# Six slots of split weight parts instead of four, splits five parts ahead, in a two-layer decoder trunk

## The chip, the cores and the metric

One core of one Trainium2 chip. The time is that of one execution on the device, in microseconds; for the kernel before, the median of three runs is 2111.45 us (2107.8 to 2112.7). Engine names follow the profile: PE is TensorE, DVE is VectorE, ACT is ScalarE, POOL is GpSimd, SP is the engine whose queue issues most loads.

## The reference, cut to what matters

256 tokens of width 2048 go through two layers. Layer 0 mixes tokens with a chunked gated linear attention (GLA), layer 1 with a sliding-window attention (SWA). Both also attend with 4 heads to 256 memory tokens. Each layer ends with an MLP of width 8192. All of it is float32.

```python
mem_n = rmsnorm(mem, mem_norm_g)
for i in range(2):
    h = rmsnorm(x, attn_norm_g[i])
    mk, mv = split(mem_n @ w_mem_kv[i])          # memory keys and values of this layer
    o_mix, xq = gla(h) if i == 0 else swa(h)
    x = x + concat(o_mix, softmax(xq mk) mv) @ w_out[i]
    x = x + square(relu(rmsnorm(x) @ w_up[i])) @ w_down[i]
return rmsnorm(x, final_norm_g)
```

## The kernel before

Weights are read once, as a list of 128 x 1024 float32 blocks (512 KB, "items", some 900 of them), and every product is made from float32r parts: a block is split into a high part `wh` (an ACT copy that rounds, L993) and a low part `wl` (a DVE subtraction, L994), and a product is high by high, high by low and low by high. An item of the up projection (`u`, L724 to L726) has 12 matmuls of 512 columns, an item of the down projection (`d`, L782 to L784) has 6, one of the attention projections (L198, L199) has 8 of 512 columns and 8 of 256.

One loop goes over the items. At step i it issues the load of item i + 8 (SP queue, a ring `wr` of 6 raw blocks), the preparation of item i + 5, the split of item i + 3 into a ring of 4 `wh` and 4 `wl` slots, then the small work that is due at this step (residual adds, norms, attention heads as generators, the hidden activations), then the matmuls of item i. A framework assigns the semaphores and the final order on each engine at build time; it may let an instruction whose inputs are due go ahead of one that stands before it in the source.

The MLP's down projection does seven eighths of its work with a seven-product scheme for 2 x 2 blocks (`FAST`): from four weight blocks B11, B12, B21, B22 it forms sums. B11 is loaded into a tile `sum` of its own and split; `first_sum` (L828, DVE) adds B12 to it, giving T1; after T1's split an accumulating DMA that POOL issues (L825) adds B22 in place, giving T2; after T2's split another adds B21, giving T4. B12's tile `b` gets B22 added by `third_sum` (L831, DVE), giving T3, from the raw block of B22 that stands in the ring. Per group of 44 items there are 16 of `u` woven with 28 of `d` (7 products, 2 halves, 2 pairs), and seven such groups per layer. In source order the two halves and pairs of T1 and T2, named T1-0 to T1-3 and T2-0 to T2-3 here, stand six or seven items apart. `hid_task` (L750 to L763) turns finished `u` into the operands `hid` of the next group's `d`.

```python
    raw[i] = wp.tile([P, 1024], F32, tag="wr", name="wr", bufs=WR)
    ...
    act.activation(hi[i][:, 0:w], r[:, 0:w], AF.Copy)
    dve.tensor_tensor(lo[i][:, 0:w], r[:, 0:w], hi[i][:, 0:w].bitcast(F32), ALU.subtract)
    if h.then:
        h.then(r)
```

Pools: `wp` holds the three rings, `tp` temporaries for the whole run (`u`, `t`, `sq`, `junk` and small ones), `S["phase"].pool` the tiles of one phase (GLA, MLP 0, SWA, MLP 1). Memory keys and values of layer 1 (`mk1`, `mv1`) are made in the GLA phase and lie in `cp`, for the whole run; those of layer 0 lie in the GLA phase's pool.

Of the kernel before, what the change touches and what calls it, by code (L numbers as in the profile page):

```python
# [20 lines left out]
EPS = 1e-5  # L21
XSCALE = 128.0 ** -0.5
WR = 6
LOAD_AHEAD = 8
PREP_AHEAD = 5
SPLIT_AHEAD = 3
MEM_AT = (10, 15)
WARM = 14

# [51 lines left out]
def trunk_kernel(ctx: ExitStack, tc: tile.TileContext, a, out):  # L81
# [150 lines left out]

    def combine(acc, name):

        u = tp.tile([P, T], F32, tag="u", name=name + "_u")
        act.activation(u, acc[:, T:2 * T], AF.Copy)
        t = tp.tile([P, T], F32, tag="t", bufs=4, name=name + "_t")
        dve.tensor_tensor(t, acc[:, 0:T], u, ALU.add)
        return t

# [12 lines left out]
            self.cm.__exit__(None, None, None)  # L253


    mkv = {1: [cp.tile([P, 4, T], F32, name="mk1"), cp.tile([P, 2, 512], F32, name="mv1")]}

    def act_item(src, first, n, key, gain, start=None):

# [47 lines left out]
    def mem_halves(layer):  # L307
        hs = []

        def mv_done(accs):  # L310
            if layer == 0:
                S["mem_r"] = S["mem_st"].spread()
            for t in range(2):
                act.activation(mkv[layer][1][:, t, :], accs[t], AF.Copy, scale=S["mem_st"].tok[:, t:t + 1])

        hs += tm_halves(f"mv{layer}", [a["w_mv"][layer, i] for i in range(8)], 512, lambda: S["ms"], mv_done)
        for c in range(4):
            def mk_done(acc, c=c):
                t = combine(acc, f"mk{layer}{c}")
                dve.tensor_tensor(mkv[layer][0][:, c, :], t, S["mem_r"], ALU.mult)  # L320

            hs += fm_halves(f"mk{layer}{c}", [a["w_mk"][layer, c, i] for i in range(2)], lambda: S["ms"], mk_done)
        return hs
# [39 lines left out]
    def gla_halves():  # L363
# [29 lines left out]
        def proj_done(job, idx):  # L393
            kind, h, j = job

            def f(acc):
                pool = S["phase"].pool
                if idx == 0:
                    S["r"] = S["st"].spread()
                    S["os"] = {}  # L400
                t = combine(acc, f"p{idx}")
                if kind == "k":
                    if j == 0:
                        S["kT", h] = pool.tile([P, 2, T], F32, tag="kT", name=f"kT{h}", bufs=2)
                    dve.tensor_tensor(S["kT", h][:, j, :], t, S["r"], ALU.mult)
                elif kind == "q":
                    if j == 0:
                        S["qT", h] = pool.tile([P, 2, T], F32, tag="qT", name=f"qT{h}", bufs=2)
                    dve.scalar_tensor_tensor(S["qT", h][:, j, :], t, 1.0 / 16, S["r"], ALU.mult, ALU.mult)
                    if j == 1:  # L410
                        tasks.append(gla_task(h))
                elif kind == "g":
                    sg = tp.tile([P, T], F32, tag="t", bufs=4, name=f"sg{idx}")
                    dve.tensor_tensor(t, t, S["r"], ALU.mult)

                    act.activation(sg, t, AF.Abs)
                    act.activation(sg, sg, AF.Exp, scale=-1.0)
                    act.activation(sg, sg, AF.Ln, bias=1.0)
                    dve.scalar_tensor_tensor(sg, t, 0.0, sg, ALU.min, ALU.subtract)
                    act.activation(sg, sg, AF.Exp)  # L420
                    dve.tensor_tensor(sg, t, sg, ALU.mult)
                    dve.scalar_tensor_tensor(sg, S["on", h][:, j, :], o_gain[:, j:j + 1], sg, ALU.mult, ALU.mult)
                    put_out(3 * h + j, sg)
                else:
                    xq = pool.tile([P, T], F32, tag="xq", name=f"xq0{h}", bufs=2)
                    dve.tensor_tensor(xq, t, S["r"], ALU.mult)
                    tasks.append(xattn_task(0, h, xq))
            return f

        for idx, job in enumerate(GLA_ORDER):  # L430
            if idx == 4:
                hs += mem_halves(0) + mem_halves(1)
            for h in fm_halves(f"p{idx}", [a["w_gla"][idx, i] for i in range(2)], lambda: S["xs"], proj_done(job, idx)):
                hs.append(h)
                if extra and idx < 4:
                    hs.append(extra.pop(0))
# [15 lines left out]
    def gla_task(h):  # L452
# [21 lines left out]
        xb = tmp("gl_xb", [P, 2])  # L474
        dve.tensor_tensor(xb, cs[:, :, 0, 127], cs[:, :, 0, 63], ALU.subtract)
        dve.tensor_scalar(xb, xb, 1.0 / 16, None, ALU.mult)
        ex = tp.tile([P, 2, P], F32, tag="t", bufs=4, name=f"ex{h}")
        for c in range(2):
            act.activation(ex[:, c, :], cs[:, c, 1, :], AF.Exp, bias=xb[:, c:c + 1], scale=1.0 / 16)
        be = e.rearrange("p (c t i) -> p c t i", c=2, t=2)  # L480
# [29 lines left out]
        for j in range(3):  # L510
# [3 lines left out]
            pe.matmul(b[:, P:T], S["v"][:, 1, col:col + P], at[:, T:T + P], start=False, stop=True,  # L514
                      skip_group_check=True)
            act.activation(on[:, j, :], b[:, 0:T], AF.Copy)
            sq.append(tp.tile([P, T], F32, tag="sq", name=f"gsq{h}{j}", bufs=2))
# [8 lines left out]
        inv_sqrt(f"go{h}", b[:, 0:T], 1.0 / 384, r, *[tp.tile([P, T], F32, tag="t", bufs=4, name=f"go{h}_{z}") for z in "vw"])  # L526
        yield
        for j in range(3):
            dve.tensor_tensor(on[:, j, :], on[:, j, :], r, ALU.mult)
# [3 lines left out]
    def start_swa():  # L533
# [12 lines left out]
        S["kd"] = [pool.tile([P, T], F32, name=f"kd{g}") for g in range(3)]  # L546
        S["vt"] = pool.tile([P, 2, 256], F32, name="vt")
        S["os"] = {}

    def kv_task(c, t):  # L550

# [146 lines left out]
    def mlp_halves(layer):  # L698
# [89 lines left out]
        def down_fast(e):  # L788


            def block(pair, u, name):
                return wd[layer, e, 2 * pair + int(name[2]) - 1, 2 * u + int(name[1]) - 1]

            def item(idx, u, pair):
# [17 lines left out]
                        later.append([1, take])  # L812

                def tile_of(kind):
                    return lambda *_: held[kind, pair, u]

                def new(kind):
                    def f():
                        held[kind, pair, u] = S["phase"].pool.tile([P, 1024], F32, tag=f"{kind}{pair}{u}",
                                                                   name=f"{kind}{layer}{e}{pair}{u}")  # L820
                        return held[kind, pair, u]
                    return f

                def plus(other):
                    return lambda raw: pool_e.dma_start(held["sum", pair, u], block(pair, u, other), accum_op=ALU.add)  # L825

                def first_sum():
                    dve.tensor_tensor(held["sum", pair, u], held["sum", pair, u], held["b12", pair, u], ALU.add)  # L828

                def third_sum(raw):  # L830
                    dve.tensor_tensor(held["b12", pair, u], held["b12", pair, u], raw, ALU.add)  # L831
# [122 lines left out]


    S["phase"] = Phase("gla")
    mkv[0] = [S["phase"].pool.tile([P, 4, T], F32, name="mk0"), S["phase"].pool.tile([P, 2, 512], F32, name="mv0")]
    S["xs"] = split_slot("A", "ax0")
    x = [[None] * 4, [None] * 4]
    tasks.append(x_task())  # L960
# [21 lines left out]
    def split(i):  # L982
# [5 lines left out]
        if h.split:  # L988
            h.split(r)
            return  # L990
        hi[i] = wp.tile([P, 1024], F32R, tag="wh", name="wh", bufs=4)
        lo[i] = wp.tile([P, 1024], F32R, tag="wl", name="wl", bufs=4)
        act.activation(hi[i][:, 0:w], r[:, 0:w], AF.Copy)  # L993
        dve.tensor_tensor(lo[i][:, 0:w], r[:, 0:w], hi[i][:, 0:w].bitcast(F32), ALU.subtract)  # L994
        if h.then:
# [84 lines left out]
def _build(a):  # L1080
    import concourse.bacc as bacc

    nc = bacc.Bacc("TRN2", target_bir_lowering=False, num_devices=1, dynamic_dma_scratch_size=8192)
    arrays, aps = {}, {}
    for name, v in a.items():
        arrays[f"in_{name}_dram"] = v
# [14 lines left out]
```

## Time and profile before

| | |
|---|---|
| median of the runs | 2111.45 us |
| the profiled execution | 2112.66 us, its span 2110.9 us |
| PE busy | 2073.6 us, 98% of the span |
| DVE, ACT busy | 1629.5 us (77%), 1252.2 us (59%) |
| granted TensorE clock of the core | 0.998 |
| data moved | 457.32 MB, mean 217 GB/s |

A matmul's busy time in the profile is the time from its start to its end in a pipeline, so the next one can start before it ends; the distance between two starts tells how fast PE goes. Idle time before an instruction and what ended it stand in brackets in a timeline.

### The profile page before, as it was taken

The page shows a single profiled execution, that of the slowest core. Times are in us where ns is not written, and L with a number is a line of the kernel's source. Part 1 is how long each engine was busy: PE and PEld are TensorE (multiplying, and loading weights), DVE is VectorE, ACT ScalarE, POOL GpSimd, SP SyncE. Part 2 cuts the span into 40 slices and gives each one's busy share as a digit, 9 for nine tenths or more (in the row PEclk, how much of TensorE's full clock was granted, in tenths as well). Part 3 has the DMA queues.
Part 4 walks back from the last instruction along what each step waited for, and adds up shares of the span by engine and source line. Part 5 has one row for each costly group of instructions (what it writes and reads, how often), then busy time and mean ns, then how long its engine had stood idle before and what let it go on. Part 6 is the DMA issues. An engine that isn't in the chain of part 4 may idle for free.

```text
span 2110.9 us, 27104 instructions
## 1 busy us (share of the span) xinstructions
PE 2073.6 (98%) x9902; PEld 1719.4 (81%) x9902; DVE 1629.5 (77%) x1993; ACT 1252.2 (59%) x1654; POOL 104.8 (5%) x138
## 2 busy tenths in 40 slices
PE   9999999999999999999999999999999999999998
PEld 9988888888787887877888887787787787877886
DVE  5655787556887988889887688557798887988975
ACT  6644666555666665666656466545566566665664
POOL 0000000000100101101000000000010100101100
PEclk9999999999999999999999999999999999999999
DMA  8856555566879879788776544575987879879773
GB/s 296 286 169 185 171 161 157 174 193 217 231 229 278 227 240 268 219 279 222 227 222 205 173 136 124 164 231 175 267 219 266 233 232 282 223 237 259 224 225 138
DMA packets 128150, 457.32 MB, mean 217 GB/s; under 512 B 14492, under 2 KB 14704, under 8 KB 128016
## 3 DMA queue, kind: packets, MB, share of 16 engines
q1 hardware_dynamic: 109872, 393.40, 56.8%
q0 software_dynamic: 16320, 58.81, 14.9%
q10 hardware_dynamic: 1824, 3.38, 0.5%
q8 instruction: 77, 1.26, 0.2%
q14 instruction: 57, 0.47, 0.1%
HBM read 453.24 MB, written 2.10 MB: 216 GB/s over the span
## 4 chain that ended last, share of the span: by engine, by line
PE 49%; issue 35%; DMA 9%; DVE 3%; ACT 2%; POOL 1%; SPq 0%; POOLq 0%; ACTq 0%; DVEq 0%
DMA sum<-in_w_down_dram 6%; PE p_acc L198 4%; PE s_acc L198 3%; PE u_acc L725 3%; PE u_acc L726 3%; PE u_acc L724 3%; DMA wr<-in_w_down_dram 3%; PE d L783 3%; PE d L782 3%; PE d L784 3%; DVE wl L994 2%; PE p_acc L199 2%; PE s_acc L199 2%; PE o_acc L224 1%; PE o_acc L225 1%
## 5 line engine op out<-in xcount | busy, mean ns | idle before, releaser
L994 DVE TENSOR_TENSOR wl<-wr,wh 128x1024 fp32r<-128x1024 f32 (+1 forms) x626 | 749.3, 1207 | 246.5 <-ACT wh L993 241.6
L993 ACT ACTIVATE wh<-wr 128x1024 fp32r<-128x1024 f32 (+1 forms) x626 | 651.6, 1047 | 435.9 <-PE o_acc L226 85.7
L725 PE MATMUL u_acc<-wl,mx 128*128 128x512 f32 x1024 | 400.3, 391 | 13.5 <-DVE wl L994 13.5
L724 PE MATMUL u_acc<-wh,mx 128*128 128x512 f32 x1024 | 399.8, 391 | 1.4 <-ACT wh L993 1.4
L726 PE MATMUL u_acc<-wh,mx 128*128 128x512 f32 x1024 | 398.7, 389 | 0.0
L993 ACT ACTIVATE wh<-sum 128x1024 fp32r<-128x1024 f32 x224 | 237.9, 1062 | 252.9 <-PE u_acc L726 160.6
L994 DVE TENSOR_TENSOR wl<-sum,wh 128x1024 fp32r<-128x1024 f32 x224 | 273.0, 1219 | 80.8 <-ACT wh L993 80.3
L783 PE MATMUL d<-wl,hid 128*128 128x512 f32 x784 | 309.7, 395 | 9.2 <-DVE wl L994 9.0
L782 PE MATMUL d<-wh,hid 128*128 128x512 f32 x784 | 308.5, 394 | 0.4 <-ACT hid L762 0.4
L784 PE MATMUL d<-wh,hid 128*128 128x512 f32 x784 | 304.5, 390 | 0.0
L725 PEld LDWEIGHTS u_acc<-wl,mx 128*128 128x128 f32 x1024 | 192.3, 188 | 58.8 <-DVE wl L994 19.5
L724 PEld LDWEIGHTS u_acc<-wh,mx 128*128 128x128 f32 x1024 | 192.1, 188 | 42.5 <-ACT wh L993 2.2
L726 PEld LDWEIGHTS u_acc<-wh,mx 128*128 128x128 f32 x1024 | 192.2, 188 | 39.9
L198 PE MATMUL p_acc<-ax,wh 128*128 128x512 f32 x512 | 183.9, 402 | 0.0
L783 PEld LDWEIGHTS d<-wl,hid 128*128 128x128 f32 x784 | 147.4, 188 | 44.5 <-DVE wl L994 15.6
L782 PEld LDWEIGHTS d<-wh,hid 128*128 128x128 f32 x784 | 147.2, 188 | 33.5 <-ACT hid L762 1.2
L784 PEld LDWEIGHTS d<-wh,hid 128*128 128x128 f32 x784 | 147.2, 188 | 32.3
L825 POOL DMA_DIRECT2D sum<-in_w_down_dram x112 | 95.6, 853 | 1496.3 <-DVE wl L994 1274.8
L199 PE MATMUL p_acc<-ax,wl 128*128 128x256 f32 x512 | 143.6, 281 | 0.0
L198 PEld LDWEIGHTS p_acc<-ax,wh 128*128 128x128 f32 x512 | 96.2, 188 | 23.7 <-ACT wh L993 1.0
L198 PE MATMUL s_acc<-ax,wh 128*128 128x512 f32 x304 | 111.3, 407 | 0.0
L831 DVE TENSOR_TENSOR b<-b,wr 128x1024 f32<-128x1024 f32 x56 | 68.3, 1220 | 45.9 <-DMA wr<-in_w_down_dram 45.9
(252 smaller groups left out, 2708.0 us busy)
## 6 DMA issues: line engine op xcount, KB each, us to landing
wr<-in_w_up_dram SPq DMA_DIRECT2D x256, 512.0 KB, 4.6
wr<-in_w_down_dram SPq DMA_DIRECT2D x144, 512.0 KB, 5.0
sum<-in_w_down_dram POOLq DMA_DIRECT2D x112, 512.0 KB, 9.7
wr<-in_w_gla_dram SPq DMA_DIRECT2D x64, 512.0 KB, 3.7
wr<-in_w_out_dram SPq DMA_DIRECT2D x64, 512.0 KB, 3.6
sum<-in_w_down_dram SPq DMA_DIRECT2D x56, 512.0 KB, 4.6
b<-in_w_down_dram SPq DMA_DIRECT2D x56, 512.0 KB, 5.1
wr<-in_w_swa_dram SPq DMA_DIRECT2D x38, 512.0 KB, 3.7
```

The costliest lines, as they stand in the source:

```text
L198: pe.matmul(acc, wh[:, k * P:(k + 1) * P], rk, start=kk == 0, stop=False, skip_group_check=True)
L199: pe.matmul(acc[:, T:2 * T], wl[:, k * P:(k + 1) * P], rk[:, 0:T], start=False, stop=kk == NK - 1, skip_group_check=True)
L724: pe.matmul(acc, hi, h, start=2 * i + k == 0, stop=False)
L725: pe.matmul(acc, hi, l, start=False, stop=False)
L726: pe.matmul(acc, lo, h, start=False, stop=2 * i + k == NK - 1)
L782: pe.matmul(acc, hi, h, start=first and c == 0, stop=False, skip_group_check=True)
L783: pe.matmul(acc, hi, l, start=False, stop=False, skip_group_check=True)
L784: pe.matmul(acc, lo, h, start=False, stop=last and c == 1, skip_group_check=True)
L825: return lambda raw: pool_e.dma_start(held["sum", pair, u], block(pair, u, other), accum_op=ALU.add)
L831: dve.tensor_tensor(held["b12", pair, u], held["b12", pair, u], raw, ALU.add)
L993: act.activation(hi[i][:, 0:w], r[:, 0:w], AF.Copy)
L994: dve.tensor_tensor(lo[i][:, 0:w], r[:, 0:w], hi[i][:, 0:w].bitcast(F32), ALU.subtract)
```

## The change

The rings of `wh` and `wl` get six slots instead of four, and an item is split five steps ahead of its matmuls instead of three, prepared seven instead of five and loaded eleven instead of eight. The raw ring keeps its 6 blocks. The room comes from four places. The temporaries `u`, `t` and `sq` move from `tp` to the pools of the phases that use them. Layer 1's memory keys and values are computed before layer 0's, written to DRAM by two DMAs from ACT's queue and read back by two at the start of the SWA phase. Their tiles share tags with those of layer 0. POOL's scratch for DMA descriptors goes from 8192 to 4096 bytes per partition. Tiles of the seven-product scheme are looked up by group (`e`) too, since the next group's loads are now issued earlier in the source.

```diff
-LOAD_AHEAD = 8
-PREP_AHEAD = 5
-SPLIT_AHEAD = 3
+LOAD_AHEAD = 11
+PREP_AHEAD = 7
+SPLIT_AHEAD = 5
+SLOTS = 6
...
-        u = tp.tile([P, T], F32, tag="u", name=name + "_u")
+        u = S["phase"].pool.tile([P, T], F32, tag="u", name=name + "_u", bufs=3)
...
-        t = tp.tile([P, T], F32, tag="t", bufs=4, name=name + "_t")
+        t = S["phase"].pool.tile([P, T], F32, tag="t", bufs=4, name=name + "_t")
...
-    mkv = {1: [cp.tile([P, 4, T], F32, name="mk1"), cp.tile([P, 2, 512], F32, name="mv1")]}
+    mkv = {}
+    dp = ctx.enter_context(tc.tile_pool(name="dp", bufs=1, space=bass.MemoryType.DRAM))
+    kept = [dp.tile([P, 1024], F32, name=f"kept_{n}") for n in ("mk", "mv")]
+
+    def new_mkv(layer):
+        pool = S["phase"].pool
+        mkv[layer] = [pool.tile([P, 4, T], F32, tag="mk", name=f"mk{layer}"),
+                      pool.tile([P, 2, 512], F32, tag="mv", name=f"mv{layer}")]
+
+    def flat(layer, i):
+        return mkv[layer][i].rearrange("p a b -> p (a b)")
+
+    def keep_mkv():
+
+        for i in range(2):
+            act.dma_start(kept[i], flat(1, i))
+
+    def fetch_mkv():
+        new_mkv(1)
+        for i in range(2):
+            act.dma_start(flat(1, i), kept[i])
...
-            if layer == 0:
+            if layer == 1:
                 S["mem_r"] = S["mem_st"].spread()
+            new_mkv(layer)
...
                 dve.tensor_tensor(mkv[layer][0][:, c, :], t, S["mem_r"], ALU.mult)
+                if (layer, c) == (1, 3):
+                    keep_mkv()
...
-                hs += mem_halves(0) + mem_halves(1)
+                hs += mem_halves(1) + mem_halves(0)
...
         S["os"] = {}
+        fetch_mkv()
...
-                    return lambda *_: held[kind, pair, u]
+                    return lambda *_: held[kind, pair, u, e]
...
-        hi[i] = wp.tile([P, 1024], F32R, tag="wh", name="wh", bufs=4)
-        lo[i] = wp.tile([P, 1024], F32R, tag="wl", name="wl", bufs=4)
+        hi[i] = wp.tile([P, 1024], F32R, tag="wh", name="wh", bufs=SLOTS)
+        lo[i] = wp.tile([P, 1024], F32R, tag="wl", name="wl", bufs=SLOTS)
...
-    nc = bacc.Bacc("TRN2", target_bir_lowering=False, num_devices=1, dynamic_dma_scratch_size=8192)
+    nc = bacc.Bacc("TRN2", target_bir_lowering=False, num_devices=1, dynamic_dma_scratch_size=4096)
```

## Rows read from the trace of the kernel before

**Rows 1.** The page: the span and part 1, busy time, share of the span and instructions of each engine.

```profile
span 2110.9 us, 27104 instructions
PE 2073.6 (98%) x9902; PEld 1719.4 (81%) x9902; DVE 1629.5 (77%) x1993; ACT 1252.2 (59%) x1654; POOL 104.8 (5%) x138
```

**Rows 2.** Who PE waited for in the whole run: total us, times, longest.

```profile
PE u_acc L725 <- DVE wl L994: 13.5, 12, 1.2
PE d L783 <- DVE wl L994: 9.0, 13, 1.6
PE v_acc L224 <- ACT wh L993: 2.2, 2, 1.3
PE u_acc L724 <- ACT wh L993: 1.4, 2, 0.7
```

**Rows 3.** Busy time by stage: GLA, SWA, MLP 0, MLP 1. After the stretch come its length, the engines' busy time with their instructions, the granted TensorE clock, the DMA share and GB/s.

```profile
60.00:460.00 400.00, 400.00 (x2101) 341.36 (x2100) 262.96 (x421) 225.97 (x382) 3.84 (x10) 1.00 0.60 185
1120.00:1410.00 290.00, 290.00 (x1571) 236.33 (x1570) 200.55 (x379) 161.11 (x337) 2.43 (x6) 1.00 0.54 163
460.00:1120.00 660.00, 647.91 (x2894) 530.38 (x2893) 553.02 (x549) 404.96 (x418) 47.78 (x56) 1.00 0.81 237
1410.00:2095.00 685.00, 672.67 (x3000) 550.36 (x2999) 571.13 (x572) 416.17 (x438) 47.79 (x56) 1.00 0.79 234
```

**Rows 4.** PE's timeline at the two waits of one group of 44 items (the second group of MLP 0): start, duration, instruction, idle before.

```profile
652.00 0.39 PE L784 MATMUL d<-wh,hid 128*128 128x512 f32 x1
652.23 0.40 PE L782 MATMUL d<-wh,hid 128*128 128x512 f32 x1
653.52 0.51 PE L783 MATMUL d<-wl,hid 128*128 128x512 f32 x1 [0.90 <-DVE wl L994]
653.87 0.40 PE L784 MATMUL d<-wh,hid 128*128 128x512 f32 x1
...
658.93 0.39 PE L724 MATMUL u_acc<-wh,mx 128*128 128x512 f32 x1
660.45 0.50 PE L725 MATMUL u_acc<-wl,mx 128*128 128x512 f32 x1 [1.13 <-DVE wl L994]
```

**Rows 5.** DVE's timeline ahead of these waits.

```profile
626.84 2.48 DVE L994 TENSOR_TENSOR wl<-sum,wh 128x1024 fp32r<-128x1024 f32 x2
...
636.12 1.23 DVE L994 TENSOR_TENSOR wl<-sum,wh 128x1024 fp32r<-128x1024 f32 x1 [0.80 <-ACT wh L993]
...
639.94 1.23 DVE L994 TENSOR_TENSOR wl<-sum,wh 128x1024 fp32r<-128x1024 f32 x1 [1.45 <-ACT wh L993]
...
651.11 1.23 DVE L831 TENSOR_TENSOR b<-b,wr 128x1024 f32<-128x1024 f32 x1 [2.47 <-DMA wr<-in_w_down_dram]
652.25 2.35 DVE L994 TENSOR_TENSOR wl<-wr,wh 128x1024 fp32r<-128x1024 f32 x2
...
655.32 1.22 DVE L994 TENSOR_TENSOR wl<-wr,wh 128x1024 fp32r<-128x1024 f32 x1
657.23 2.02 DVE L763 TENSOR_TENSOR hid<-q,hid 128x1792 fp32r<-128x1792 f32 x1 [0.69 <-ACT hid L762]
659.17 1.22 DVE L994 TENSOR_TENSOR wl<-wr,wh 128x1024 fp32r<-128x1024 f32 x1
```

**Rows 6.** ACT's timeline (the copies of T2-2 and T2-3), and SP's issue of the load that L831 waits for.

```profile
635.03 1.06 ACT L993 ACTIVATE wh<-sum 128x1024 fp32r<-128x1024 f32 x1 [1.56 <-DMA sum<-in_w_down_dram]
638.84 1.06 ACT L993 ACTIVATE wh<-sum 128x1024 fp32r<-128x1024 f32 x1 [2.75 <-DMA sum<-in_w_down_dram]
...
643.46 0.33 SPq L976 DMA_DIRECT2D wr<-in_w_down_dram  x1
```

**Rows 7.** POOL's timeline: issues of accumulating DMAs, the first two of T1 (T1-2, T1-3), the others of T2.

```profile
625.48 0.85 POOL L825 DMA_DIRECT2D sum<-in_w_down_dram  x1 [3.15 <-DVE wl L994]
628.34 0.85 POOL L825 DMA_DIRECT2D sum<-in_w_down_dram  x1 [2.02 <-DVE wl L994]
629.61 0.85 POOL L825 DMA_DIRECT2D sum<-in_w_down_dram  x1 [0.42 <-DVE wl L994]
633.80 0.85 POOL L825 DMA_DIRECT2D sum<-in_w_down_dram  x1 [3.34 <-DVE wl L994]
```

**Rows 8.** Busy time in one group, from its first accumulating DMA to that of the next group; columns as in rows 3.

```profile
619.20:705.65 86.45, 84.43 (x377) 69.10 (x377) 74.99 (x75) 53.26 (x55) 6.82 (x8) 1.00 0.84 243
```

**Rows 9.** DVE's timeline in the later part of the same group: its idle times there.

```profile
669.84 1.23 DVE L994 TENSOR_TENSOR wl<-sum,wh 128x1024 fp32r<-128x1024 f32 x1 [1.44 <-ACT wh L993]
...
673.93 1.23 DVE L994 TENSOR_TENSOR wl<-sum,wh 128x1024 fp32r<-128x1024 f32 x1 [1.13 <-ACT wh L993]
...
679.40 1.23 DVE L994 TENSOR_TENSOR wl<-sum,wh 128x1024 fp32r<-128x1024 f32 x1 [1.37 <-ACT wh L993]
...
683.77 0.69 DVE L809 TENSOR_TENSOR x<-d,x 128x512 f32<-128x512 f32 x1 [1.77 <-PE d L784]
```

**Rows 10.** ACT's waits in the group of rows 8.

```profile
ACT wh L993 <- PE u_acc L726: 11.1, 7, 1.7
ACT wh L993 <- DMA sum<-in_w_down_dram: 6.1, 3, 2.8
```

**Rows 11.** The page, parts 3 and 6: the queue of POOL's transfers (packets, MB, share of 16 engines), and the accumulating DMA (count, KB, median us to landing).

```profile
q0 software_dynamic: 16320, 58.81, 14.9%
...
sum<-in_w_down_dram POOLq DMA_DIRECT2D x112, 512.0 KB, 9.7
```

**Rows 12.** The busiest 50 us of the SWA phase (columns as in rows 3), and the DMAs that ACT's queue issues for x (min, median, max ns of an issue).

```profile
1250.00:1300.00 50.00, 50.00 (x327) 39.29 (x326) 42.62 (x109) 32.11 (x90) 0.00 (x0) 1.00 0.44 127
...
L297 ACTq DMA_DIRECT2D x<-in_x_tok_dram x8: 334/334/460, 1.3 to 21.1; - x8
```

More of the change, by code (lines that the diff above doesn't have):

```diff
@@ L412, in f @@
                 elif kind == "g":
-                    sg = tp.tile([P, T], F32, tag="t", bufs=4, name=f"sg{idx}")
+                    sg = S["phase"].pool.tile([P, T], F32, tag="t", bufs=4, name=f"sg{idx}")
                     dve.tensor_tensor(t, t, S["r"], ALU.mult)
@@ L476, in gla_task @@
         dve.tensor_scalar(xb, xb, 1.0 / 16, None, ALU.mult)
-        ex = tp.tile([P, 2, P], F32, tag="t", bufs=4, name=f"ex{h}")
+        ex = S["phase"].pool.tile([P, 2, P], F32, tag="t", bufs=4, name=f"ex{h}")
         for c in range(2):
@@ L516, in gla_task @@
             act.activation(on[:, j, :], b[:, 0:T], AF.Copy)
-            sq.append(tp.tile([P, T], F32, tag="sq", name=f"gsq{h}{j}", bufs=2))
+            sq.append(S["phase"].pool.tile([P, T], F32, tag="sq", name=f"gsq{h}{j}", bufs=2))
             act.activation(sq[j], b[:, 0:T], AF.Square)
@@ L525, in gla_task @@
         r = tmp("gl_r", [P, T])
-        inv_sqrt(f"go{h}", b[:, 0:T], 1.0 / 384, r, *[tp.tile([P, T], F32, tag="t", bufs=4, name=f"go{h}_{z}") for z in "vw"])
+        inv_sqrt(f"go{h}", b[:, 0:T], 1.0 / 384, r, *[S["phase"].pool.tile([P, T], F32, tag="t", bufs=4, name=f"go{h}_{z}") for z in "vw"])
         yield
@@ L814, in tile_of @@
                 def tile_of(kind):
-                    return lambda *_: held[kind, pair, u]
+                    return lambda *_: held[kind, pair, u, e]
                 def new(kind):
                     def f():
-                        held[kind, pair, u] = S["phase"].pool.tile([P, 1024], F32, tag=f"{kind}{pair}{u}",
+                        held[kind, pair, u, e] = S["phase"].pool.tile([P, 1024], F32, tag=f"{kind}{pair}{u}",
                                                                    name=f"{kind}{layer}{e}{pair}{u}")
-                        return held[kind, pair, u]
+                        return held[kind, pair, u, e]
                     return f
                 def plus(other):
-                    return lambda raw: pool_e.dma_start(held["sum", pair, u], block(pair, u, other), accum_op=ALU.add)
+                    return lambda raw: pool_e.dma_start(held["sum", pair, u, e], block(pair, u, other), accum_op=ALU.add)
                 def first_sum():
-                    dve.tensor_tensor(held["sum", pair, u], held["sum", pair, u], held["b12", pair, u], ALU.add)
+                    dve.tensor_tensor(held["sum", pair, u, e], held["sum", pair, u, e], held["b12", pair, u, e], ALU.add)
                 def third_sum(raw):
-                    dve.tensor_tensor(held["b12", pair, u], held["b12", pair, u], raw, ALU.add)
+                    dve.tensor_tensor(held["b12", pair, u, e], held["b12", pair, u, e], raw, ALU.add)
                 if name == "B11":
@@ L956, in trunk_kernel @@
     S["phase"] = Phase("gla")
-    mkv[0] = [S["phase"].pool.tile([P, 4, T], F32, name="mk0"), S["phase"].pool.tile([P, 2, 512], F32, name="mv0")]
     S["xs"] = split_slot("A", "ax0")
```

## The prediction

> **What bounds the kernel now.** I read the page first, then PE's waits, then the stages one by one, then the timelines of one group of 44 items on each engine. The page says that PE is busy for 98% of the span [rows 1]. So a change can win only what PE waits for, and PE's waits have few causes: 25 of the 29 are for a `wl` that DVE had not finished, 22.5 us in all, and the rest are two short waits for `wh` and two in the first microseconds [rows 2]. By stage they lie in one place. In the GLA and SWA phases PE is busy for the whole stretch, in the two MLPs it lacks 12.1 and 12.3 us [rows 3]. The granted clock is 1.00 in all four, so nothing is to be had or lost there.
>
> The timelines show why DVE is late in an MLP. Each group has up to two waits, some 7 us apart [rows 4]. Going back from them on DVE [rows 5]: at 651.11 it runs the last `third_sum`, after 2.47 us of waiting for the raw block, and two splits stand behind it (652.25). SP issued that block's load at 643.46 [rows 6], when a slot of the raw ring came free, and it landed 7.6 us later. The slot came late because the splits before it were late: ACT's copies of T2-2 and T2-3 stood still for 1.56 and 2.75 us until accumulating DMAs landed [rows 6]. The one for T2-3 was issued at 628.34 [rows 7], right after T1-3's split, and landed at about 638.8. From the end of T1-3's split (626.84 + 2.48 less an overlapping third split, about 628.1) to the start of T2-3's copy there are 10.8 us, whatever DVE does. Four `d` and two `u` lie between, which PE does in 11.0 us (at 0.23 us from start to start [rows 4], `d` is 1.38 us, `u` 2.76 us), and copy and subtraction take 2.3 us more. So this chain of latency eats some 2 us of whatever DVE is ahead; the late block and `hid` (2.02 us at 657.23, with 0.69 of idle) eat the rest. It is a shortage of cover in one third of the group, not of throughput: DVE is busy for 75.0 of 86.5 us [rows 8], and later in the same group it stands idle because the four slots are full [rows 9]; ACT stands 11.1 us waiting for PE to free one [rows 10].
>
> **The slots, the main term.** How late is DVE? PE wanted the first late `wl` at 652.23 + 0.23 = 652.46 and started on it at 653.52, 1.06 us late; the next matmul started 0.35 us after that instead of 0.23. The second was wanted at 659.16 and started at 660.45, 1.29 us late although PE had already lost 1.2 [rows 4]. Without any wait the second `wl` would be 2.5 us late. That is the cover that this group lacks.
>
> With six slots the copy of item k may start when PE ends item k - 6 instead of k - 4. The two items between are a `d` and a `u` in most places, 1.38 + 2.76 = 4.1 us, and two `d` in some, 2.8 us. Both are more than 2.5 us. DVE must have idle time to run that far ahead: in the later part of the group it has 1.44 + 1.13 + 1.37 + 1.77 = 5.7 us [rows 9], more than 4.1. And over a group without waits, 86.5 less 2.6 = 83.9 us, DVE's 75.0 us and the idle time that slots can't take away (2.47 for the block, 0.80 + 1.45 for T2, 0.69 for `hid` [rows 5]; 5.4 us) make 80.4 us. It still fits, with 3.5 us to spare. So I take it that the waits for `wl` go.
>
> Their price: 22.5 us of idle time [rows 2]. A recorded idle time counts from the modelled end of the matmul before, so a wait cost 1.06 where 0.90 is recorded, and 0.12 more on the next start: 0.28 us for each of 25, 7.0 us. The two waits of `u` for `wh` I take for ACT behind a full ring too; by the same count 1.4 + 0.6 = 2.0 us. Together 31.5 us; the waits at the start (2.2 us) stay, as the first loads set them.
>
> I don't take all of it. The groups differ, and in the first group of each MLP the ring starts from another state; the margin is 1.6 us where `d` and `u` alternate and 0.3 us where two `d` follow each other. I leave 3.5 us, a tenth, standing: 28 us are won. The lower bound of this term is nothing (the chain only moves), the upper 31.5.
>
> **Loads earlier in the source.** SP's loads keep their order, and the raw ring keeps 6 blocks, so a load still waits for the split of the sixth raw block before it. It comes earlier only because that split does. Nothing is added: 0 us, with the last-mentioned load moved forward along with DVE. If it did not move, the 2.47 us at L831 would grow by what DVE gained; this is the second rival.
>
> **Memory keys through DRAM.** Four DMAs of 512 KB on ACT's queue, at 0.33 us to issue each [rows 12]: 1.3 us of ACT, which is busy for 32 of 50 us even in the densest part of SWA. The write must wait for DVE's last product of `mk`, with ACT's next copy queued behind it, and that copy has five items of lead; layer 0's values, which reuse the tile, come eight items later. The read is issued when the SWA phase opens, and the first head that needs it comes four items and two steps after. An item of the attention phases has 16 matmuls, at 400 us / 2101 [rows 3] some 3 us, so six of them, 18 us, cover it. A transfer of this size lands in 4 to 10 us here [rows 11]. Taken: 0. If the cover were gone: each 1 MB at SWA's 127 GB/s for a 0.44 share, that is 290 GB/s when full, is 3.6 us, twice, 7 us at most.
> The Trainium skill speaks against counting it as free: DMA: Bandwidth & Descriptors, section "Issuing engines are not separate DMA queues", says that transfers issued by ScalarE run on the same 16 DMA engines as SyncE's and interleave with them. By that the weights' loads pay for the 2 MB, and the sum would be 21 us won instead of 28; the DMA share of 0.44 to 0.60 in these phases is why I don't follow it here, and no run yet shows it.
>
> **Temporaries, names, order of memory layers.** The same instructions on the same engines; only addresses and the pool change. A phase's tiles now lie over those of the phase before, as others did; all their readers are done by then. 0 us, with 1 us per phase change (four of them) as the bound if one has to wait.
>
> **Half the descriptor scratch.** POOL's issue takes 0.85 us with up to four accumulating DMAs in flight (those of 625.48 to 633.80, the first landing at about 635.0 [rows 6, 7]), and what ended its idle time was always DVE. So no shortage shows. 0 us taken; what a shortage would cost is the third rival.
> By the Trainium skill (DMA: Bandwidth & Descriptors, sections "Terms" and "SWDGE vs HWDGE vs iDMA") a descriptor has 16 bytes and these rings lie in the reserved part of SBUF, so 4096 bytes are an estimated 256 entries, against 9 packets per engine and transfer from the page's count of 16320 for some 118 transfers: 4 in flight would use 36. No run shows what a full ring does.
>
> **The sum.** 2112.66 us less 28 is 2084.7 for an execution like the profiled one, which stands 1.2 us above the median of the runs; less these, 2083.5, say 2084.
>
> **The rivals.**
> *Part of it only.* The framework orders DVE again at build time. If it puts `third_sum` or `hid` in front of more splits than now, or DVE cannot use the 5.7 us, half of the waits stay: 2112 - 14 = 2098. For it: the row at 651.11, where an instruction that waits stands in front of two splits [rows 5]. Against it: the lead now has 1.6 us to give.
> *It moves with the chain.* T1 to T2 stays 10.8 us, the block's 7.6 us too. If DVE's extra lead is spent on waiting there each time, PE's waits stay as they are: 2111. Against it: DVE's idle time is elsewhere [rows 9] and a chain that starts 4.1 us earlier ends 4.1 us earlier.
> *Slower, by the scratch.* If the halved room holds fewer than four transfers, each issue waits for a landing: four of T1 at 10 us apart instead of 1.3 to 4. T2-3's data then come some 20 us later; 6 us of cover leave 14 us, 14 groups, about 200 us: 2280. It decides at fewer than four in flight; with room for three it would be nearer to 3 us a group, 42 against 28, 2126.
> *Slower, by order.* Small work of a step now stands behind two more splits. In the densest SWA stretch DVE is busy for 42.6 of 50 us [rows 12]; if it falls behind there, probabilities reach PE late, by up to two splits (2.4 us), for 12 pairs of heads at two places each: 58 us against 28 gained, 2142. It decides when DVE is more than the three steps behind that the generators leave. Against it: PE doesn't wait once there now, and DVE has 15% left.
>
> **How the numbers follow.** Waits mostly gone (won 18 to 33 us, 2079 to 2094): 0.62. Part only (5 to 18 us, 2094 to 2106): 0.17. Within 0.2%, 4.2 us, which is about what a measurement of this kernel can tell: 0.09, the second rival with some mishaps. Slower: 0.12, of which the scratch 0.04. The range from 2078 to 2104 holds the first case and nearly all of the second. Faster 0.79, same 0.09, slower 0.12.
>
> **What would show it.** PE's waits for `wl` should fall from 25 to a few, and PE's matmuls in the MLPs keep 0.23 us from start to start; the MLPs should give nearly all of the gain, GLA and SWA none. ACT's waits for PE stay, since full slots are the normal state. DVE's wait at L831 and ACT's for accumulating DMAs may stay or grow without PE waiting. POOL's issue should stay at 0.85 us. The prediction is wrong if PE waits in SWA, for `hid`, or for `wl` at the same two places.

## The result: 1% faster, and what stands behind it

| | before | after |
|---|---|---|
| median of the runs | 2110.76 us (2107.8 to 2112.7, 4 runs) | 2090.57 us (2087.34 to 2091.28, 4 runs) |
| the profiled execution, its span | 2112.66, 2110.9 us | 2087.34, 2085.6 us |

The ratio is 0.9903, with a 95% interval from 0.9885 to 0.992. The sign was forecast, and the time lies in the range, but 6.6 us above the forecast: 20.2 us were won by the medians (25.3 by the two profiled executions), not 28.

The page of after, the span and part 1, answers to [rows 1]:

```profile
span 2085.6 us, 27140 instructions
PE 2068.6 (99%) x9902; PEld 1719.9 (82%) x9902; DVE 1625.0 (78%) x1993; ACT 1240.2 (59%) x1654; POOL 104.9 (5%) x138
```

The engines do the same work, so the gain is time that PE no longer stands idle. Who PE waited for in after (total us, times, longest), against [rows 2]; line numbers have moved by 24 or 25 in the MLP, L750 here is L725 there, L808 is L783:

```profile
PE v_acc L225 <- ACT wh L1017: 2.3, 2, 1.9
PE d L808 <- DVE wl L1018: 2.3, 4, 0.8
PE u_acc L750 <- DVE wl L1018: 1.9, 2, 1.0
PE warm L118 <- DVE ones L109: 1.1, 1, 1.1
```

25 waits for `wl` with 22.5 us have become six with 4.2, and the two of `u` for `wh` are gone. The stages (GLA, SWA, MLP 0, MLP 1; columns as in [rows 3]) show PE busy all through GLA and SWA, as before, and lacking 2.1 and 2.5 us in the MLPs in place of 12.1 and 12.3. The granted clock stays at 1.00:

```profile
60.00:460.00 400.00, 400.00 (x2106) 341.87 (x2105) 263.75 (x422) 226.73 (x384) 3.80 (x10) 1.00 0.60 188
1110.00:1400.00 290.00, 290.00 (x1572) 236.26 (x1571) 199.24 (x380) 162.50 (x340) 2.43 (x6) 1.00 0.53 166
460.00:1110.00 650.00, 647.91 (x2904) 532.46 (x2903) 553.67 (x552) 400.35 (x419) 47.88 (x56) 1.00 0.81 242
1400.00:2070.00 670.00, 667.55 (x2985) 548.20 (x2983) 564.76 (x565) 406.00 (x431) 47.84 (x56) 1.00 0.79 236
```

Idle time doesn't show the whole price of a late `wl`. A better measure of an MLP is its length in the trace, from the start of its first matmul of `u` to the start of its last of `d`. This is worked out from the start times of PE's matmuls, for both MLPs together (each rounded to 0.1 us before they are added), and stands below for every kernel. GLA is the time from PE's first instruction to the first `u`, SWA that from the end of MLP 0 to the start of MLP 1. Beside them stand the recorded waits for `wl` and what DVE waited for the raw block in front of `third_sum`. The last column is read off DVE's order, for the last `third_sum` of each group: how many splits run after it though the source has them before it, the split of its own block among them. All of it is of the profiled executions.

| kernel | MLPs, us | GLA | SWA | PE for `wl` | DVE at `third_sum` | splits that `third_sum` is ahead of |
|---|---|---|---|---|---|---|
| before | 1379.0 | 467.9 | 241.9 | 22.5, 25 times | 45.9, 17 times | 3 |
| after | 1354.9 | 467.0 | 242.3 | 4.2, 6 times | 51.6, 16 times | 4 |
| `room_only` | 1375.2 | 466.9 | 242.3 | 19.2, 23 times | 48.7, 23 times | 3 |
| `slots_not_order` | 1352.9 | 466.7 | 242.1 | 1.9, 3 times | 55.7, 17 times | 4 |
| `five_slots` | 1346.7 | 468.6 | 242.3 | none | 18.9, 16 times | 2 |
| `raw_ring` | 1358.2 | 466.5 | 242.3 | 1.0, twice | 1.8, twice | 6 (11 in the first group of an MLP) |
| `pinned_before` | 1348.0 | 467.7 | 241.9 | none | none | 0 |
| `swap_before` | 1348.2 | 468.1 | 241.9 | none | none | 0 (1 in the first group of an MLP) |
| `pinned_room` | 1348.1 | 466.7 | 242.3 | none | none | 0 |
| `pinned_slots3` | 1345.9 | 466.7 | 242.1 | none | none | 0 |
| `pinned_five` | 1346.0 | 468.7 | 242.3 | none | none | 0 |
| `pinned_six` | 1346.0 | 466.8 | 242.3 | none | none | 0 |

So 24.1 us of the 25.3 between the profiled executions lie in the MLPs, and the MLPs had 33.0 us to give (1379.0 less 1346.0). After leaves 8.9 of them. GLA's length goes with the code of that phase: 467.7 to 468.1 us in the old kernel's three, 466.5 to 467.0 in the changed ones with four or six slots. The 468.6 and 468.7 with five slots are a matter of TensorE's clock in these two executions: from 9 to 14 us the granted clock is 0.66 in both, and 1.00 in `pinned_six` and in before. The two are 1.8 and 1.9 us behind `pinned_six` by 15 us, and still so at 281 us.

Why are 8.9 us left? DVE's timeline in one group of MLP 0 of after, at 807 to 825 us (start, duration, instruction, idle before and what ended it), against [rows 5]:

```profile
807.43 1.22 DVE L1018 TENSOR_TENSOR wl<-wr,wh 128x1024 fp32r<-128x1024 f32 x1
811.71 1.23 DVE L856 TENSOR_TENSOR b<-b,wr 128x1024 f32<-128x1024 f32 x1 [3.07 <-DMA wr<-in_w_down_dram]
812.86 3.49 DVE L1018 TENSOR_TENSOR wl<-wr,wh 128x1024 fp32r<-128x1024 f32 x3
...
821.90 2.03 DVE L788 TENSOR_TENSOR hid<-q,hid 128x1792 fp32r<-128x1792 f32 x1 [0.70 <-ACT hid L787]
823.84 2.35 DVE L1018 TENSOR_TENSOR wl<-b,wh 128x1024 fp32r<-128x1024 f32 x2
```

PE's timeline of after behind that:

```profile
825.11 0.50 PE L808 MATMUL d<-wl,hid 128*128 128x512 f32 x1 [0.84 <-DVE wl L1018]
825.45 0.39 PE L809 MATMUL d<-wh,hid 128*128 128x512 f32 x1
```

And SP's timeline, the issue of the block's load:

```profile
804.13 0.33 SPq L1000 DMA_DIRECT2D wr<-in_w_down_dram  x1
```

The last `third_sum` of the group (L856, which was L831) still waits for its raw block, now 3.07 us, and now three splits stand behind it, where two stood before [rows 5], beside the split of its own block (818.51 to 819.73 here, 655.32 there). The three run back to back at 812.86, though ACT had made the last of their copies by 807.95. SP issued the block's load at 804.13 and it landed 7.6 us later, as before [rows 6]. In every group DVE's new lead is spent at this one instruction: the idle in front of it is 3.1 to 4.5 us in after's 14 groups, 2.2 to 3.5 in before's (from the end of the DVE instruction ahead to its start). The lead can be counted, from the end of an item's split to the start of the first matmul that wants its `wl`. The last item split ahead of this `third_sum` has 2.7 to 6.3 us in after's groups, the first one behind it 0.1 to 2.1, and in ten of the 14 groups one of the next eleven items is left with 0.1 us, no more than at a recorded wait. After `hid` at 821.90 the next `wl` comes just too late for PE at 825.11. The six recorded waits with what hangs on them make 5.9 of the 8.9 us; the rest are starts that come late by some 0.1 us each, without recorded idle time.

### The profile page after: what moved, and what is told of

The parts are those of the page before. It is cut to its first block, busy times and chain, and to the rows that moved or that the text cites. A ratio compares the mean times of both kernels' runs of the same rounds, so it can differ in the third digit from the quotient of the medians.

```text
span 2085.6 us, 27140 instructions
## 1 busy us (share of the span) xinstructions
PE 2068.6 (99%) x9902; PEld 1719.9 (82%) x9902; DVE 1625.0 (78%) x1993; ACT 1240.2 (59%) x1654; POOL 104.9 (5%) x138
## 4 chain that ended last, share of the span: by engine, by line
PE 63%; issue 23%; DMA 6%; DVE 6%; ACT 1%; POOL 1%; SPq 0%; ACTq 0%; DVEq 0%; POOLq 0%
PE u_acc L750 6%; PE u_acc L751 6%; PE u_acc L749 6%; PE d L808 5%; PE d L807 5%; PE d L809 5%; PE p_acc L199 4%; DMA sum<-in_w_down_dram 4%; PE s_acc L199 3%; DVE wl L1018 3%; PE p_acc L200 2%; DMA wr<-in_w_down_dram 2%; PE s_acc L200 2%; PE o_acc L225 1%; PE o_acc L226 1%
## 5 line engine op out<-in xcount | busy, mean ns | idle before, releaser
L750 PE MATMUL u_acc<-wl,mx 128*128 128x512 f32 x1024 | 399.0, 390 | 1.9 <-DVE wl L1018 1.9
L808 PE MATMUL d<-wl,hid 128*128 128x512 f32 x784 | 309.3, 395 | 2.3 <-DVE wl L1018 2.3
L750 PEld LDWEIGHTS u_acc<-wl,mx 128*128 128x128 f32 x1024 | 192.3, 188 | 42.7 <-DVE wl L1018 3.0
L808 PEld LDWEIGHTS d<-wl,hid 128*128 128x128 f32 x784 | 147.4, 188 | 34.6 <-DVE wl L1018 5.8
L856 DVE TENSOR_TENSOR b<-b,wr 128x1024 f32<-128x1024 f32 x56 | 68.3, 1220 | 51.6 <-DMA wr<-in_w_down_dram 51.6
```

Of the source, the lines that this page charges most:

```text
L750: pe.matmul(acc, hi, l, start=False, stop=False)
L808: pe.matmul(acc, hi, l, start=False, stop=False, skip_group_check=True)
L856: dve.tensor_tensor(held["b12", pair, u, e], held["b12", pair, u, e], raw, ALU.add)
```

## The experiments

The theory after this look: DVE's order sets the waits. In source order `third_sum` stands behind the split of its own block, item 26 of the group of 44 (counted from 0). At build time it was put further ahead on DVE, and ready splits wait with it. The rivals: the slots themselves fall short (too few, or too few raw blocks), or the chain of accumulating DMAs is late whatever DVE does.

**`room_only`: after, with the rings and distances of before.**

```diff
-LOAD_AHEAD = 11
-PREP_AHEAD = 7
-SPLIT_AHEAD = 5
-SLOTS = 6
+LOAD_AHEAD = 8
+PREP_AHEAD = 5
+SPLIT_AHEAD = 3
+SLOTS = 4
```

> All that makes the room (memory keys through DRAM, temporaries in their phase, half the descriptor scratch, layer 1's memory work first), but four slots and splits, preparation and loads 3, 5 and 8 ahead as before. Theory (cover): the gain comes from the slots alone, so this stands at the time before, 2111 us, within 4 us, and PE waits some 25 times for wl. Rival (order): any change of the source gives the engines another order at build time, and that is what helped: nearer to 2090 us. Rival (cost): the DRAM round trip or the halved scratch costs something that the slots hid: 2115 to 2125 us.

Measured: 2107.9 us (2105.94 to 2111.39, 10 runs), ratio 0.999, from 0.9981 to 0.9999. PE's waits:

```profile
PE u_acc L750 <- DVE wl L1018: 13.8, 12, 1.2
PE d L808 <- DVE wl L1018: 5.4, 11, 1.0
PE u_acc L749 <- ACT wh L1017: 1.4, 2, 0.7
```

The DRAM round trip, the temporaries and the halved scratch cost nothing that can be measured; the pattern of waits is that of [rows 2]. The 2.6 us are hardly more than the interval; `pinned_room` comes back to them.

**`five_slots`: less of the same change.**

```diff
-LOAD_AHEAD = 11
-PREP_AHEAD = 7
-SPLIT_AHEAD = 5
-SLOTS = 6
+LOAD_AHEAD = 10
+PREP_AHEAD = 6
+SPLIT_AHEAD = 4
+SLOTS = 5
```

> The changed kernel with five slots and splits four ahead (prepared 6, loaded 10). Theory (cover): one more slot gives 1.4 or 2.8 us of cover, 2.1 us in the mean, where the second late wl of a group lacked 2.5 us: about half of the 25 waits stay, shorter; 2095 to 2102 us. Rival (threshold): one slot is enough, 2090 us as with six. Rival (no throughput): cover is spent on waiting, 2108 us or more.

Measured: 2080.81 us (2079.12 to 2080.86), ratio 0.9857, from 0.9842 to 0.9872. Five slots are 10 us faster than six; I had expected the opposite. PE waits for no `wl` at all. DVE's timeline of `five_slots` in the same group:

```profile
811.26 0.68 DVE L836 TENSOR_TENSOR x<-x,d 128x512 f32<-128x512 f32 x1
812.56 1.22 DVE L856 TENSOR_TENSOR b<-b,wr 128x1024 f32<-128x1024 f32 x1 [0.62 <-DMA wr<-in_w_down_dram]
813.70 0.68 DVE L780 TENSOR_TENSOR q<-q 128x512 f32<-128x512 f32 x1
814.30 2.35 DVE L1018 TENSOR_TENSOR wl<-wr,wh 128x1024 fp32r<-128x1024 f32 x2
```

`third_sum` comes two splits later in DVE's order here: of the three that stand behind it in after, two run ahead of it (the last two of those just before 811.26) and one behind. It waits 0.62 us instead of 3.07. Here one slot less and a later place in the order come with shorter waits. That fits the theory and speaks against "too few slots", but slots and order still change together. In the MLPs of the profiled executions five slots win 8.2 us on six.

**`slots_not_order`: six slots, split, prepared and loaded as far ahead in the source as in before.**

```diff
-LOAD_AHEAD = 11
-PREP_AHEAD = 7
-SPLIT_AHEAD = 5
+LOAD_AHEAD = 8
+PREP_AHEAD = 5
+SPLIT_AHEAD = 3
```

> The changed kernel with six slots, but splits, preparation and loads only 3, 5 and 8 ahead in the source. If the slots set how far ACT and DVE run ahead and the framework moves a split ahead of blocked small work, this is as fast as the changed kernel, 2087 to 2093 us. If the place in the source binds (a split stands behind the small work of the step three before its matmuls, which waits for PE), the lead stays near 3 us and the time near 2105 to 2111 us. I hold the second for somewhat likelier: 2103 us.

Measured: 2084.15 us (2083.13 to 2084.93), ratio 0.9874, from 0.986 to 0.9889: faster than after, against my expectation, and below the rival's. Who PE and DVE waited for:

```profile
PE u_acc L750 <- DVE wl L1018: 1.5, 2, 1.0
PE d L808 <- DVE wl L1018: 0.4, 1, 0.4
...
DVE b L856 <- DMA wr<-in_w_down_dram: 55.7, 17, 4.9
```

The gain of the slots needs no earlier split in the source: six slots let ACT and DVE run ahead as they come free. DVE's timeline in the group shown for after:

```profile
810.58 1.23 DVE L856 TENSOR_TENSOR b<-b,wr 128x1024 f32<-128x1024 f32 x1 [3.19 <-DMA wr<-in_w_down_dram]
811.73 1.22 DVE L1018 TENSOR_TENSOR wl<-wr,wh 128x1024 fp32r<-128x1024 f32 x1
...
813.46 1.22 DVE L1018 TENSOR_TENSOR wl<-wr,wh 128x1024 fp32r<-128x1024 f32 x1
...
815.19 1.22 DVE L1018 TENSOR_TENSOR wl<-wr,wh 128x1024 fp32r<-128x1024 f32 x1
```

`third_sum` stands where it stands in after, ahead of the same three splits and its own; only residual adds now run between them. So it is the number of slots that brought it there, not the distances. The total wait at it is the longest of all kernels, and the lead behind it falls as low as in after (its least value is 0.1 to 1.1 us in the 14 groups, 0.1 to 1.0 in after). The MLPs are 6.9 us longer than in `pinned_six`, against 8.9, though only 1.9 us of PE's waits are recorded. What makes these 2 us isn't shown.

**`raw_ring`: four slots, but ten raw blocks, loaded twelve ahead.**

```diff
-WR = 6
-LOAD_AHEAD = 11
-PREP_AHEAD = 7
-SPLIT_AHEAD = 5
-SLOTS = 6
+WR = 10
+LOAD_AHEAD = 12
+PREP_AHEAD = 5
+SPLIT_AHEAD = 3
+SLOTS = 4
```

> The same 16 KB per partition spent on the raw ring instead: 10 raw blocks, four slots, splits 3 ahead, loads 12 ahead. Theory (cover): the block that L831 (now another line) waits for comes in time, DVE's 2.5 us of idle there go, and these are as much as the cover that a group lacked; the waits for accumulating DMAs stay. PE's waits fall to less than ten, 2090 to 2098 us. Rival (accumulating DMAs are the cause, the late block only follows from them): 2107 us or more. Rival (the room alone): as room_only.

Measured: 2090.04 us (2087.91 to 2092.3), ratio 0.9903, from 0.9886 to 0.9919. With the block there in time the wait at the last `third_sum` is gone in all 14 groups, and so are PE's waits of the later groups, with the old four slots. `third_sum` stands even further ahead of its place than in before (six splits against three), so the order by itself costs PE little in the later groups when the block is there: the block's lateness is a cause of before's waits. That the time is only that of after has another reason: compared matmul by matmul with `pinned_six`, all but 0.5 us of its 12.2 us in the MLPs arise in the first group of each MLP, where PE's order differs too. PE waits there for `wh` (4.6 us recorded in both MLPs together) and `wl` (1.0 us), and part of it is the clock (see the last section).

**`pinned_six`: the whole change, and `third_sum` kept in its place.**

```diff
-                    dve.tensor_tensor(held["b12", pair, u, e], held["b12", pair, u, e], raw, ALU.add)
+                    tc.keep_in_program_order(dve.tensor_tensor(held["b12", pair, u, e], held["b12", pair, u, e], raw, ALU.add))
```

> The changed kernel (six slots, five ahead) with third_sum held at its place in DVE's order, behind the split of its own block, instead of where the framework moves it. Theory (order): in the changed kernel the last third_sum of a group stands in front of three splits and waits 3.1 to 4.9 us for its block; with five slots it stands in front of one and waits about 1 us. Held back it waits for nothing that its own split doesn't wait for, PE's waits for wl go, and the time is that of five slots, 2079 to 2083 us. Rival (six slots or five ahead cost in themselves): it stays at 2086 to 2091 us.

Measured: 2078.45 us (2078.29 to 2078.68), ratio 0.9848, from 0.9833 to 0.9862. DVE's timeline in the group shown for after:

```profile
808.39 2.35 DVE L1018 TENSOR_TENSOR wl<-wr,wh 128x1024 fp32r<-128x1024 f32 x2
810.66 1.22 DVE L856 TENSOR_TENSOR b<-b,wr 128x1024 f32<-128x1024 f32 x1
811.79 0.68 DVE L836 TENSOR_TENSOR x<-x,d 128x512 f32<-128x512 f32 x1
...
818.98 2.03 DVE L788 TENSOR_TENSOR hid<-q,hid 128x1792 fp32r<-128x1792 f32 x1
```

The splits run first, the block is there when `third_sum` comes, at 810.66, and nothing waits up to `hid`. PE has no wait for `wl` in the whole run, and the lead of the same eleven items never falls below 4.2 us in the 14 groups. One line is worth 12.1 us on top of the change (9.0 by the profiled executions, of which 8.9 lie in the MLPs). PE runs its matmuls in the same order as in after. On DVE some other instructions stand elsewhere too, here and in the other pairs with and without the line, since the framework orders them anew; what is shown is the order with `third_sum` held, not that instruction alone.

**`pinned_before`: that line alone, in the old kernel.**

```diff
-                    dve.tensor_tensor(held["b12", pair, u], held["b12", pair, u], raw, ALU.add)
+                    tc.keep_in_program_order(dve.tensor_tensor(held["b12", pair, u], held["b12", pair, u], raw, ALU.add))
```

> The kernel before, four slots and all else as it was, with third_sum held at its place in DVE's order. Theory (order): the third_sum that waits 2.5 us for its block no longer stands in front of two splits, which were wanted 1.06 and, without the first wait, 2.5 us too late; most of the 25 waits go without any slot, 2085 to 2095 us. Rival (slots): four slots are too few whatever the order, since the accumulating DMAs and hid take the cover; 2102 us or more.

Measured: 2082.79 us (2081.53 to 2084.18), ratio 0.9868, from 0.9853 to 0.9883, better than I had expected. Without a slot, a raw block or a byte of room, one line wins 27.7 us, more than the whole change. PE's waits, and ACT's for the accumulating DMAs:

```profile
PE u_acc L724 <- ACT wh L993: 1.4, 2, 0.7
PE d L782 <- ACT hid L762: 0.4, 2, 0.2
...
ACT wh L993 <- DMA sum<-in_w_down_dram: 44.1, 24, 2.8
```

ACT still waits 44.1 us for accumulating DMAs (46.4 in before), and PE for no `wl`. The chain from T1 to T2 that I had put beside the late block doesn't delay PE by itself. Four slots are just enough, though: the least lead among these items is 0.4 or 0.5 us in 12 of the 14 groups.

**`swap_before`: the accumulating DMAs' chain eased in the old kernel.** The product of T2 changes places with the product of B22 in the list.

```diff
+        (S4, "B22", 1, False, [(0, 1, -1)]),
         (S2, "T2", 0, False, [(0, 1, -1)]),
-        (S4, "B22", 1, False, [(0, 1, -1)]),
```

> The kernel before with the products S4 x B22 and S2 x T2 exchanged in the list, so that four more items of d lie between T1's split and T2's: some 25 us instead of 11 to 14 for the accumulating DMA to land. third_sum may land elsewhere in DVE's order. Theory (both chains): ACT no longer waits 6 us a group for accumulating DMAs, DVE has 2 us more of cover, and half or more of the waits go, 2087 to 2098 us. Rival (only the late block counts): 2106 us or more.

Measured: 2083.68 us (2081.99 to 2085.34), ratio 0.9872, from 0.9857 to 0.9887. PE's only wait of the MLPs beside `hid`:

```profile
PE u_acc L724 <- ACT wh L993: 1.4, 2, 0.7
```

The time is below both ranges, and it doesn't separate the two chains: ACT's waits for accumulating DMAs are gone, but so is DVE's wait at L831. B22 now comes earlier in the list, and `third_sum` stands in its place in 12 of the 14 groups, one split ahead in the two others. It only shows that another order of the work, with neither of the two waits, ends at the same 1348 us.

**`pinned_five`: five slots and the line.** The constants of `five_slots` and the line of `pinned_six`.

```diff
...
-SPLIT_AHEAD = 5
-SLOTS = 6
...
+SPLIT_AHEAD = 4
+SLOTS = 5
...
```

> Five slots, four ahead, third_sum held at its place. With five slots PE did not wait for wl at all, so there is nothing left to gain: 2079 to 2082 us, DVE's wait at third_sum (about 1 us a group) gone or moved to ACT. If holding instructions back costs DVE time that PE feels, 2084 us or more.

Measured: 2078.52 us (2078.31 to 2080.28), ratio 0.9847, from 0.9831 to 0.9864. The same as with six.

**`pinned_room`: four slots, the freed room, and the line.** The constants of `room_only` and the line of `pinned_six`.

```diff
...
-SPLIT_AHEAD = 5
-SLOTS = 6
...
+SPLIT_AHEAD = 3
+SLOTS = 4
...
```

> The kernel after with four slots and the old distances (8, 5, 3), and third_sum kept in its place. It tells what of the 4.3 us between the pinned old kernel (2082.8) and the pinned six slots (2078.5) is the freed room and what is slots. Room by itself won 2.6 us without the pin. Theory: the two waits for wh at the starts of the MLPs (0.85 us each) stay with four slots, so 2080.2, from 2079 to 2081.5. Rival: the room is worth nothing and the slots all: 2082 to 2083.5. Other rival: slots are worth nothing once the order is held: 2078 to 2079.

Measured: 2082.19 us (2080.41 to 2083.6), ratio 0.9864, from 0.9846 to 0.9883. This is `pinned_before`'s time, in the MLPs to 0.1 us (1348.1 and 1348.0), so the first rival is right: the room by itself is worth nothing there, and at most the 1.0 us that GLA is shorter. What `room_only` won (3.8 us in its MLPs) goes with its waits for `wl`, which the line removes anyway; why they were shorter there stays open.

**`pinned_slots3`: six slots, split three ahead in the source, and the line.** The constants of `slots_not_order` and the line of `pinned_six`.

```diff
...
-SPLIT_AHEAD = 5
...
+SPLIT_AHEAD = 3
...
```

> The same with six slots, still split three ahead. Theory: the wait for wh at the start of an MLP goes with the slots, not with the source distance: 2078.5, as with five slots and as with the whole change. Rival: the distance matters, and it stays at the time of four slots, 2080 or above. PE should have no wait for wl in an MLP in either kernel.

Measured: 2077.73 us (2077.67 to 2081.17), ratio 0.9845, from 0.9829 to 0.9862. Its only waits of PE are these:

```profile
PE v_acc L225 <- ACT wh L1017: 1.3, 1, 1.3
PE warm L118 <- DVE ones L109: 1.1, 1, 1.1
PE d L807 <- ACT hid L787: 0.2, 1, 0.2
```

With `third_sum` held, the distance in the source is worth nothing, and more slots win 2.1 us in the MLPs (1348.1 to 1345.9 to 1346.0): the two waits of `u` for `wh` (1.4 recorded, 0.28 more for each by the prediction's count) make 2.0 of them. By the medians the gap is 3.7 to 4.5 us, with intervals that overlap.

## Why the prediction was right, and where it failed

**What bounds the kernel: right.** The gain lies in the MLPs, and PE's waits for `wl` were what there was to win. The price was nearly right too: I summed 31.5 us, and the MLPs can give 33.0. The 0.28 us per wait beside the recorded idle holds: after's six waits have 4.2 us recorded, and against the same matmuls in `pinned_six` those six starts and the one behind each are 5.9 us late, 0.28 for each.

**The slots: the step that failed is the one on DVE's order.** I wrote that the 5.4 us of idle time which slots can't take away stay as they were, and that the block's load comes forward along with DVE. DVE's order was built anew, and with six slots `third_sum` went in front of three splits instead of two, earlier against its block (`slots_not_order` has it there with the old distances). The wait there grew from 45.9 to 51.6 us, and most of the lead that six slots gave was handed back at that place. This is the rival "part only", by the mechanism it named; it was priced at 14 us left standing and left 8.9. By its time the result still lies in the likeliest case: the lead was large enough to carry most of a longer wait. How far the framework would move `third_sum` the prediction left open, and nothing in the runs shows a rule in it: four, five and six slots put it three, two and four splits ahead. That it came out no worse is luck. I gave it 0.17 and 28 us to the likeliest case, whose allowance of 3.5 us should have been 8.9.

**What I took for a shortage of cover was mostly an order.** I read the row at 651.11 [rows 5] as one of several things that eat a lead and asked how much lead would cover them. The question asked only in a rival was why an instruction that waits stands in front of two that don't. `pinned_before` answers it: with `third_sum` in its place, four slots suffice for all but 2 us. In the same way the chain from T1 to T2, worked out there to 10.8 us, is real but harmless: in `pinned_before` ACT waits for it as long as before, and PE doesn't.

**Two terms of the comparison.** The forecast for an execution like the profiled one was 2084.7 us, and it came to 2087.34. The other 3.2 us are the scatter of the runs: after's profiled execution is its fastest, where before's stood 1.2 us above the median that the forecast started from.

**Memory keys through DRAM: right at 0.** GLA, which writes them, got 0.9 us shorter, and SWA, which reads them, 0.4 us longer. The list of after's DMA issues has the round trip (KB, median us to landing) beside a weight load of the SWA phase:

```profile
wr<-in_w_swa_dram SPq DMA_DIRECT2D x38, 512.0 KB, 3.6
...
kept_mv<-mv ACTq DMA_DIRECT2D x1, 512.0 KB, 3.5
kept_mk<-mk ACTq DMA_DIRECT2D x1, 512.0 KB, 4.5
mk<-kept_mk ACTq DMA_DIRECT2D x1, 512.0 KB, 4.9
mv<-kept_mv ACTq DMA_DIRECT2D x1, 512.0 KB, 4.7
```

The Trainium skill's rule that ACT's transfers share the DMA engines with SP's (DMA: Bandwidth & Descriptors, "Issuing engines are not separate DMA queues") would have made this 7 us, by the prediction's estimate from [rows 12]. No run shows that price: `room_only`, which has the round trip, is not slower than before, and the DMA share in SWA is 0.53.

**Temporaries, scratch, order in SWA: right at 0.** POOL's row in part 5 of after:

```profile
L850 POOL DMA_DIRECT2D sum<-in_w_down_dram x112 | 95.7, 855 | 1470.2 <-DVE wl L1018 1259.1
```

The issue takes 0.855 us with half the scratch, against 0.85 [rows 7], and DVE ends most of its idle time; PE doesn't wait once in the SWA stretch. Neither of the slower rivals came. For the scratch the trace of before had only the row on POOL's issue; `room_only` settles it, with half the scratch and no time lost.

**What would show it.** Of the signs named, the few waits left for `wl`, the gain in the MLPs alone, ACT's waits for PE that stay (those for `u` and `d` fell from 347 to 246 us), and POOL's issue came as written. That the wait at L831 might grow without PE waiting was half right: it grew, and PE waited. One sign of being wrong showed in small: in the first group of each MLP PE still waits for `wl` at a place where it waited in before (0.91 and 1.03 us, for a `u`). The other four waits stand one item behind the second old place, at a `d`. PE also waits once for `hid`, 0.2 us, as it did twice in before; my count of 29 waits left those two and one in the warm-up out.

## What to carry to other kernels

Before buying buffers for a late engine, look on its timeline for an instruction that waits for a transfer with ready ones behind it, and ask who put it there: here holding one such instruction in source order won 27.7 us, and two more slots without it 20.2. Whoever changes buffers or look-ahead under a framework that orders instructions itself should compare the engines' order before and after, since a constant can move a waiting instruction further ahead (the number of slots did it here: five beat six by 10 us). The best kernels here are five or six slots with that line, at 2078 us, 1.5% below before; the line alone gives 1.3%.

## What the runs showed of the hardware

The accumulating DMAs, which POOL issues, take about twice as long to land as SP's plain loads of the same size. Whether the adding or POOL's queue makes it, no run tells. The page of after, part 6:

```profile
sum<-in_w_down_dram POOLq DMA_DIRECT2D x112, 512.0 KB, 10.2
...
sum<-in_w_down_dram SPq DMA_DIRECT2D x56, 512.0 KB, 5.7
b<-in_w_down_dram SPq DMA_DIRECT2D x56, 512.0 KB, 5.0
```

A short stop of PE can cost more than itself. In `raw_ring`, PE waits 1.15 and 0.52 us within 3 us in the first group of MLP 0, and the granted clock of the 4 us after that is 0.59. PE's timeline of `raw_ring`:

```profile
520.64 0.74 PE L749 MATMUL u_acc<-wh,mx 128*128 128x512 f32 x2 [1.15 <-ACT wh L1017]
521.90 0.50 PE L750 MATMUL u_acc<-wl,mx 128*128 128x512 f32 x1 [0.52 <-DVE wl L1018]
...
524.10 0.63 PE L808 MATMUL d<-wl,hid 128*128 128x512 f32 x1
524.53 0.63 PE L749 MATMUL u_acc<-wh,mx 128*128 128x512 f32 x1
```

The stretches of `raw_ring` from 522 us on (columns of [rows 3]):

```profile
522.00:526.00 4.00, 3.95 (x10) 2.84 (x11) 2.51 (x2) 1.72 (x3) 0.00 (x0) 0.59 0.45 131
526.00:540.00 14.00, 12.83 (x52) 9.18 (x51) 11.99 (x13) 8.53 (x8) 1.79 (x2) 0.99 0.40 78
```

Matmuls start 0.43 us apart there (524.10 to 524.53) instead of 0.23, PE at the lower of its two levels, 1.2 GHz, for most of these 4 us; then it is back at 2.4 GHz. The same comes in the first group of MLP 1 (0.76 over 1448 to 1454 us, after a wait of 1.15 us). In before, waits of 0.90 and 1.13 us, 7 us apart [rows 4], left the clock at 1.00 [rows 8]. Nor is a stop enough by itself: at its start `pinned_five` has the same 2.1 us of recorded waits for `wh` as `pinned_six`, and only in `pinned_five` does the granted clock fall, to 0.66 over 9 to 14 us.
